# Twelve of a hybrid encoder's input-projection blocks by fifteen products, six more in front, all kept in DRAM until used

## The chip, the cores and the metric

The kernel runs on one core of a Trainium2 chip. Its engines are TensorE (PE, with its weight loads shown as PEld), VectorE (DVE), ScalarE (ACT), GpSimd (POOL) and SyncE (SP), which issues most of the DMA transfers. The metric is the device time of one execution in microseconds (us), the median of several runs. Before the change it is 1644.96 us, of three runs at 1642.6, 1644.96 and 1649.06.

## The reference

One layer of a streaming encoder is computed in float32 for 1024 prompt frames and 32 sample frames, 1056 token columns in all, with a model width of 1024:

```python
h = rmsnorm(x, g_mix) * (1 + sc1) + sh1
u = h @ w_in
qa, ka, va, qm, km, vm, om, ip, fp, ga, gm = split(u)
ya = band_attention(qa, ka, va, rel_bias)      # 8 heads x 64, own chunk and 8 before
conv = silu(causal_conv4(concat(qm, km)))      # width-4 convolution along the tokens
hm = mlstm_chunkwise(conv_q, conv_k, vm, ip, fp, C0, n0, m0)   # 4 heads x 128, a recurrence
ym = head_rmsnorm(hm, mh_gain) * sigmoid(om)
merged = sigmoid(ga) * (ya @ w_br_att) + sigmoid(gm) * (ym @ w_br_mlstm)
x = x + gt1 * (merged @ w_out)
h2 = rmsnorm(x, g_ffn) * (1 + sc2) + sh2
x = x + gt2 * ((silu(g) * up) @ w_down)        # g, up = split(h2 @ w_gate_up)
y = rmsnorm(x, g_final)
```

sh1, sc1, gt1, sh2, sc2, gt2 come from `silu(c) @ w_ada + b_ada`, one row for the prompt and one for the sample. Besides y, the new keys and values, the last rows ahead of the convolution, and the mLSTM state are outputs.

## The kernel before, in words

**Tiling.** All activations lie transposed: model width on the partitions, tokens along the free axis. The 1056 tokens are cut into three thirds of 352 columns (`TILES`, line 24). A block is 128 columns of a weight; its result is one 128 x 1056 row. A matmul multiplies 128 x 128 of the weight with 128 x 352 tokens. Float32 accuracy comes from three passes (`PASSES`, line 41) over high and low halves: weights are split by `split_to` (389 to 395: a copy on ACT gives the high half, a subtraction on DVE or POOL the low one), tokens h too. So a `unit` (421), one block times one third, is 8 x 3 = 24 matmuls, and a block 72.

**Order.** PE, ACT, DVE and POOL run in the order in which the program is written. `Weights` (55) loads raw blocks ahead on SP's queue and splits up to `ahead` blocks before use. `Side` (102) is the pacing: `unit` calls `side.tick()` after every six matmuls, and a job started with so many steps over so many ticks advances by its share. In this way a generator such as `attention(hp)` (638, 22 steps) or `mlstm(pr)` (992, 26 steps, two for each 128 tokens) is laced between the matmuls of plain blocks. The list `segs` gives each segment its plain blocks and its generator:

- k0, v0, q0 alone (k0 and v0 by `first_units`, line 440, which runs two blocks at once while h is made slice by slice)
- attention(0) beside k, v, q of the next pair of heads and 2 gates; attention(1) likewise; attention(2) beside k, v, q and 4 gates
- attention(3) beside vm0 and the convolution blocks 0, 4, 1, 5
- mlstm(0) beside vm1 and the convolution blocks 2, 6, 3, 7
- mlstm(1), then `branch_operands`, beside four output-gate blocks (`om_block`, 1168) and 8 gates

`ada_rest` (1129), the rest of the modulation, is a side job of 160 steps spread over 495 ticks from the second segment on. Gate rows are stored to DRAM by SP (`gate_block`, 590) and loaded in the merge.

**An mLSTM pass.** `first` (1017) makes scores, mask and weighted keys of the next 128 tokens, `scaled` (1088) scales the numerator of the pass before, `weigh` (1042) weighs scores, `second` (1046) computes numerator and new state C and then the scale: reciprocal on DVE (1079), squares on ACT (1082), mean and power on POOL (1084, 1085). `third` (1093) transposes the result.

**Fifteen products.** The FFN's up projection already has a cheaper form. Instead of 3 x 2 x 3 block products (three weight rows, two halves of the model width, three thirds of tokens), fifteen products of sums of weights with sums of tokens are made, each of 4 x 3 = 12 matmuls; `fifteen_products` adds them into three rows. The token sums, called forms, are made first: `early_forms` (48 sums shared by DVE and POOL at line 1563, 24 low halves at 1576) beside a few plain blocks, then `late_forms` (20 low halves) in the first ten products. `times` holds the matmul of line 1726. For these stages the PSUM pools mm and ps (line 428's results, scores) are closed and psb opened, eight banks.

## Time and profile before

| what | value |
|---|---|
| three runs | 1642.6, 1644.96, 1649.06 us |
| profiled execution, its own time | 1642.54 us |
| its span | 1640.6 us |
| granted TensorE clock, mean | 0.995 |
| DMA, mean over the span | 117 GB/s |
| start to the first block's matmuls | 48.4 us |
| k0 and v0 (`first_units`) | 48.4 to 73.6 us |
| q0 | 73.6 to 88 us |
| attention 0, 1, 2, 3 | to 176, 263, 373, 473.6 us |
| mLSTM first and second half, up to the last gates | to 568.5 and 730 us |
| merge, output projection, norm, three plain FFN blocks | to about 1018 us |
| fifteen products of the FFN | 1018 to 1373 us |
| down projection and final norm | to 1640.6 us |

Busy times of an engine are read as shares of a window: an engine with 100% sets its length, one with 60% may still set it by an order of waits. "Idle before" a group of instructions names the instruction that ended the wait. Matmul ends are modelled, so a wait of PE is seen best as a gap between groups.

### The profile page before, as it was taken

What the parts mean: (1) busy time and instruction counts of PE and PEld (TensorE: products, weight loads), DVE (VectorE), ACT (ScalarE), POOL (GpSimd) and SP (SyncE); (2) the same over time, 40 slices, a digit from 0 to 9 for tenths busy, and PEclk for the clock granted to TensorE, in tenths of its full rate; (3) what the DMA queues carried; (4) which work ended last, traced back from release to release, by engine and by line L of the source; (5) the groups of instructions that cost most, each with busy time, mean ns of one, the idle gap of its engine ahead of it and who ended that gap; (6) DMA issues with size and microseconds to landing.
All of it is one profiled execution on the core that took longest, in us unless ns stands there. A gap on an engine that the chain in (4) does not pass through costs nothing.

```text
span 1640.6 us, 27517 instructions
## 1 busy us (share of the span) xinstructions
PE 1589.7 (97%) x10324; PEld 1566.7 (95%) x10324; DVE 1121.0 (68%) x2100; ACT 780.8 (48%) x1732; POOL 535.7 (33%) x540
## 2 busy tenths in 40 slices
PE   7989999999999999999999998999999999999997
PEld 6989999999999999999999988999999999999997
DVE  6756564546776744546655689889888986698754
ACT  3456454543455544444434645454545444444443
POOL 1234333333332311000012155566565742233101
PEclk9999999999999999999999999999999999999999
DMA  9732323232222332584453211313222236427453
GB/s 344 251 98 75 111 75 106 67 126 75 84 83 78 67 94 66 131 273 152 128 151 109 91 53 39 105 53 104 79 82 88 78 102 216 141 65 238 134 157 123
DMA packets 210326, 192.45 MB, mean 117 GB/s; under 512 B 10570, under 2 KB 180530, under 8 KB 209170
## 3 DMA queue, kind: packets, MB, share of 16 engines
q1 hardware_dynamic: 205970, 188.60, 36.8%
q10 hardware_dynamic: 4224, 2.10, 0.4%
q8 instruction: 81, 1.33, 0.4%
q14 instruction: 51, 0.42, 0.1%
HBM read 152.19 MB, written 41.63 MB: 118 GB/s over the span
## 4 chain that ended last, share of the span: by engine, by line
PE 79%; DVE 8%; ACT 3%; issue 2%; DMA 1%; POOL 1%; DVEq 0%; POOLq 0%; ACTq 0%
PE mm L428 35%; PE psb L1726 24%; PE psb L2082 5%; PE mm L825 3%; PE psb L1967 3%; PE psV L725 2%; PE psS L667 1%; DVE wsp L395 1%; PE psT L694 1%; DVE s L395 1%; DVE s L1576 1%; DVE s L1989 1%; DVE sl L1563 1%; DVE st L681 1%; PE psV L1059 1%
## 5 line engine op out<-in xcount | busy, mean ns | idle before, releaser
L428 PE MATMUL mm<-s,wsp 128*128 128x352 f32 x4104 | 690.4, 324 | 5.8 <-DVE t L1657 1.9
L428 PEld LDWEIGHTS mm<-s,wsp 128*128 128x128 f32 x4104 | 656.8, 188 | 9.0 <-DVE stg L518 2.3
L1726 PE MATMUL psb<-s,wsp 128*128 128x352 f32 x2544 | 422.0, 323 | 11.4 <-DVE s L1989 5.5
L1726 PEld LDWEIGHTS psb<-s,wsp 128*128 128x128 f32 x2544 | 410.9, 189 | 14.4 <-issue 6.1
L395 DVE TENSOR_TENSOR wsp<-wraw,wsp 128x512 fp32r<-128x512 f32 (+1 forms) x284 | 246.0, 884 | 136.0 <-ACT wsp L394 134.2
L394 ACT ACTIVATE wsp<-wraw 128x512 fp32r<-128x512 f32 x340 | 201.5, 617 | 147.6 <-PE psb L1726 84.5
L687 POOL TENSOR_SCALAR st<-st,mx 128x640 f32<-128x640 f32 (+5 forms) x72 | 57.0, 791 | 193.7 <-DVE mx L686 179.5
L1141 DVE SCALAR_TENSOR_TENSOR t<-wa,cmix,t 128x512 f32<-128x512 f32 x112 | 88.8, 797 | 8.9 <-DMA wa<-in_w_ada_dram 8.5
L395 POOL TENSOR_TENSOR wsp<-wraw,wsp 128x512 fp32r<-128x512 f32 x56 | 73.8, 1339 | 52.4 <-ACT wsp L394 52.0
L2082 PE MATMUL psb<-s,wsp 128*128 128x352 f32 x528 | 86.7, 324 | 0.0
L2082 PEld LDWEIGHTS psb<-s,wsp 128*128 128x128 f32 x528 | 84.7, 188 | 0.0
L681 DVE CUSTOM_DVE_ANT_0 st<-psS,bias 128x640 f32<-128x640 f32 (+5 forms) x72 | 44.5, 618 | 57.8 <-PE psS L667 44.9
L1726 PE MATMUL psb<-x,wsp 128*128 128x352 f32 x432 | 80.2, 325 | 2.3 <-DVE x L1576 2.3
L682 ACT ACTIVATE st<-st,mx 128x640 f32<-128x640 f32 (+5 forms) x72 | 47.9, 666 | 67.5 <-DVE mx L681 67.5
L1676 POOL TENSOR_TENSOR t<-t,sl 128x352 f32<-128x352 f32 x18 | 17.4, 969 | 185.3 <-ACT sl L1674 185.3
L1726 PEld LDWEIGHTS psb<-x,wsp 128*128 128x128 f32 x432 | 71.5, 189 | 2.8 <-DVE x L1576 2.8
L701 ACT ACTIVATE pT<-psT 128x640 fp32r<-128x640 f32 (+3 forms) x80 | 38.7, 494 | 72.1 <-PE psT L694 55.1
L1764 DVE TENSOR_TENSOR t<-t,psb 128x352 f32<-128x352 f32 x120 | 60.4, 512 | 5.2 <-PE psb L1726 4.8
L1361 POOL TENSOR_TENSOR wraw<-wraw 128x512 f32<-128x512 f32 x25 | 37.1, 1482 | 76.8 <-DVE wsp L395 75.8
L706 DVE TENSOR_TENSOR pT<-psT,pT 128x640 fp32r<-128x640 f32 (+3 forms) x80 | 44.0, 559 | 20.5 <-ACT pT L701 20.4
L1361 POOL TENSOR_TENSOR wraw<-wraw,raw 128x512 f32<-128x512 f32 x33 | 55.8, 1704 | 0.9
L825 PE MATMUL mm<-s,s 128*128 128x264 f32 (+3 forms) x432 | 54.9, 283 | 0.0
(340 smaller groups left out, 2334.2 us busy)
## 6 DMA issues: line engine op xcount, KB each, us to landing
wraw<-in_w_in_dram SPq DMA_DIRECT2D x40, 512.0 KB
wraw<-in_w_gate_up_dram SPq DMA_DIRECT2D x33, 512.0 KB
wa<-in_w_ada_dram SPq DMA_DIRECT2D x64, 256.0 KB
wraw<-in_w_down_dram SPq DMA_DIRECT2D x32, 512.0 KB
a_d<-t SPq DMA_DIRECT2D x22, 528.0 KB
g_d<-t SPq DMA_DIRECT2D x16, 528.0 KB
x<-xres SPq DMA_DIRECT2D x16, 528.0 KB
t<-g_d SPq DMA_DIRECT2D x16, 528.0 KB
```

The lines of the kernel that those rows point to most:

```text
L394: act.activation(dst[:, 0], src, AF.Copy)
L395: eng.tensor_tensor(dst[:, 1], src, f(dst[:, 0]), op=ALU.subtract)
L428: pe.matmul(pt[:, :hi - lo], wt[(w0 + k) // 4][:, a, (w0 + k) % 4], xt[k][:, b, lo:hi], start=(k == 0 and q == 0), stop=(k == n - 1 and q ...
L681: dve.tensor_tensor_reduce(so, sv, bi, -1.0, 3.0e38, ALU.add, ALU.min, mx[:n, 1:2])
L687: pool.tensor_scalar(st[:n, :w], st[:n, :w], mx[:n, 3:4], 1.0, op0=ALU.mult, op1=ALU.mult)
L825: pe.matmul(pt[:n, :wd], hs[k][:, a, i * P:i * P + n], whl[b][:, k, :wd], start=(k == 0 and q == 0), stop=(k == KD - 1 and q == 2))
L1141: dve.scalar_tensor_tensor(ac[:, c], wa, cmix[:, c, k:k + 1], ac[:, c], op0=ALU.mult, op1=ALU.add)
L1361: pool.tensor_tensor(a(dst), a(x), a(y), op=op)
L1726: pe.matmul(acc, wt[:, a, k], x[k][:, b], start=(start and not onto and k == 0 and q == 0), stop=(stop and k == 3 and q == 2), skip_group_ ...
L1764: dve.tensor_tensor(c, c, y, op=ALU.add if sign > 0 else ALU.subtract)
L1967: pe.matmul(acc, wt[k // 4][:, u, k % 4], piece_of[k, i][:, v], start=(k == 0 and q == 0), stop=(k == KP - 1 and q == 2))
L2082: pe.matmul(acc, wt[(k - k0) // 4][:, u, (k - k0) % 4], piece_of[k, 2][:, v], start=(k == 0 and q == 0), stop=(k == NF - 1 and q == 2))
```

## The change

24 blocks of w_in get a new place and a new way: convolution 2, 6, 3, 7, the four output-gate blocks and the 16 merge gates. Their rows go to DRAM (`u_d`, `o_d`, `g_d`), now stored by ACT's queue.

- Six of them come first as plain blocks, two in `first_units` and four beside the forms of h (`Tokens`, the FFN's helper made a class). For these, each normalised x gets its shift added in place (`whole_x`), and one third of it is stored to DRAM (`h_d`), since the forms will overwrite that third of the split h.
- Twelve follow as four times fifteen products (720 matmuls for 864).
- Then the PSUM pools are changed back, the thirds of h are loaded and split again, and k0, v0, q0 begin.
- The six gates that are left stand in the two mLSTM segments: two behind vm1, four beside mlstm(1).
- The segments of attention 0 to 2 hold k, v, q alone. Convolution rows 2, 6, 3, 7 and the output gate are loaded from DRAM. `ada_rest` has a number of steps for each segment, from the first on.
- `on_pool` says where weights' low halves are made: on DVE in the front and in the last segment, on POOL between.

```diff
+    def whole_x(j):
+        x = xns[j]
+        for c, a, b in col_segments(0, T):
+            act.activation(x[:, a:b], x[:, a:b], AF.Identity, bias=sh1[:, c, j:j + 1])
+        act.dma_start(h_d[j], x[:, thirds[1 + j // 4]])
...
-                split_to(t[:, :, :n], raw[:, 4 * i:4 * i + n], pool if (W.done or home is slots) and not hm_n[1] else dve)
+                split_to(t[:, :, :n], raw[:, 4 * i:4 * i + n], pool if on_pool[0] else dve)
...
+    def raw_block(c0, dst, home=None, order=(0, 1, 2), last=lambda: None):
+        w = w_cols(c0, home)
+        def run():
+            raw = tmpt()
+            for lo, hi, pt in units(w, order, last):
+                act.activation(raw[:, lo:hi], pt, AF.Copy)
+            W.advance()
+            act.dma_start(dst, raw)
...
+    def conv_loaded(b):
+        xin, dst = conv_in(b)
+        for c, x, y in col_segments(0, T):
+            sp.dma_start(xin[:, x + 3 + 3 * c:y + 3 + 3 * c], u_d[b][:, x:y])
+        for _ in range(3):
+            yield
+        yield from conv_tail(b, xin, dst)
...
+    def load_convs(bs, ticks, delay):
+        late_conv.append(side.start(chain(*map(conv_loaded, bs)), len(bs) * CONV_STEPS, ticks, delay))
...
+    kept = [(QM + b * P, u_d[b]) for b in (2, 6, 3, 7)] + [(OM + b * P, o_d[b]) for b in range(4)] + gates
+    NFRONT, NROWS = 6, 12
...
-        (nothing, b_qkv(0), None, 0),
-        (nothing, mix(b_qkv(1), b_gates(0, 2)), lambda: attention(0), ATT_STEPS),
-        (nothing, mix(b_qkv(2), b_gates(2, 4)), lambda: attention(1), ATT_STEPS),
-        (nothing, b_qkv(3) + b_gates(4, 8), lambda: attention(2), ATT_STEPS),
+        (nothing, b_qkv(0), None, 0, 36),
+        (nothing, b_qkv(1), lambda: attention(0), ATT_STEPS, 20),
+        (nothing, b_qkv(2), lambda: attention(1), ATT_STEPS, 20),
+        (nothing, b_qkv(3), lambda: attention(2), ATT_STEPS, 20),
         (mlstm_setup, [vm_block(0), conv_block(0), conv_block(4), conv_block(1), conv_block(5)],
-         lambda: attention(3), ATT_STEPS),
-        (open_mls, [vm_block(1), conv_block(2), conv_block(6), conv_block(3), conv_block(7)],
-         lambda: mlstm(0), ML_STEPS),
-        (nothing, [om_block(b) for b in range(4)] + b_gates(8, 16),
-         lambda: chain(mlstm(1), conv_rows(), branch_operands()), ML_STEPS + BR_STEPS + 3),
+         lambda: attention(3), ATT_STEPS, 56),
+        (open_mls, [vm_block(1)] + rest[:2], lambda: mlstm(0), ML_STEPS, 14),
+        (om_loads, rest[2:],
+         lambda: chain(mlstm(1), conv_rows(), branch_operands()), ML_STEPS + BR_STEPS + 3, 0),
...
+    tk = Tokens(hs, xq)
+    first_units([run.w for run in front[:2]])
+    on_pool[0] = False
+    W.ahead = 4
+    tk.job = side.start(tk.early(), 9, 10)
+    def start_late():
+        side.drain(tk.job)
+        tk.job = side.start(tk.late_forms(), 24, 24)
+    for run in front:
+        run()
...
+        fifteen_products(tk, x, rows, third_done)
...
+    for j in range(KD):
+        sp.dma_start(back[j], h_d[j])
+    W.ahead = 2
+    on_pool[0] = True
+    for run in segs[0][1][:2]:
+        first[id(run.w), 0] = unit(run.w, 0, hs, *TILES[0])
+    for j in range(KD):
+        split_to(hs[j][:, :, thirds[1 + j // 4]], back[j])
...
-            ada = side.start(ada_rest(), ADA_STEPS, 495)
+        ada[1] = ada_steps / ticks
...
-            delay = 13 if i >= 5 else 0
+            delay = 13 if i == 5 else 4 if i == 6 else 0
             job = side.start(gen(), steps, ticks - delay - 4, delay)
+        if i == 6:
+            on_pool[0] = False
```

The changed kernel's instructions stand in a new order. Line numbers of the changed kernel differ: its plain matmul is line 448 (428 before), transposes of attention 720 (694), scores 693 (667), mLSTM 1057, 1059, 1087 to 1092 (1026, 1028, 1056 to 1061).

PE, in an attention of wide steps, before: one step of attention (transposes psT, scores psS, values psV) and the plain matmuls mm of a block, three to a row, that follow. `s` are tiles of split activations, `wsp` split weights.

```order
L694 MATMUL psT_3227<-ident,st_3091 128x128 x5
L667 MATMUL psS_3235<-s_1842,s_2458 128x320
L667 MATMUL psS_3235<-s_1842,s_722 128x320
L667 MATMUL psS_3235<-s_1842,s_2458 128x320
L667 MATMUL psS_3235<-s_1842,s_722 128x320
L725 MATMUL psV_3174<-pT_3156,s_2237 128x256 x4
L428 MATMUL mm_3213<-s_582,wsp_2960 128x352 x3
L428 MATMUL mm_3213<-s_607,wsp_2960 128x352 x3
L428 MATMUL mm_3213<-s_633,wsp_2960 128x352 x3
L428 MATMUL mm_3213<-s_665,wsp_2960 128x352 x3
L428 MATMUL mm_3274<-s_479,wsp_2959 128x352 x3
L428 MATMUL mm_3274<-s_505,wsp_2959 128x352 x3
```

The same place of the changed kernel, one step to the next:

```order
L720 MATMUL psT_4674<-ident,st_4616 128x128 x5
L693 MATMUL psS_4682<-s_3656,s_4213 128x320
L693 MATMUL psS_4682<-s_3656,s_2686 128x320
L693 MATMUL psS_4682<-s_3656,s_4213 128x320
L693 MATMUL psS_4682<-s_3656,s_2686 128x320
L751 MATMUL psV_4664<-pT_4646,s_4252 128x256 x4
L448 MATMUL mm_4715<-s_473,wsp_4465 128x352 x3
L448 MATMUL mm_4715<-s_499,wsp_4465 128x352 x3
L448 MATMUL mm_4715<-s_527,wsp_4465 128x352 x3
L448 MATMUL mm_4715<-s_555,wsp_4465 128x352 x3
L720 MATMUL psT_4731<-ident,st_4653 128x128 x5
```

After the step, six rows of plain matmuls (18) or more stood before; now four rows (12) stand between one step and the next.

PE, in the second half of mLSTM, before: the second part of a pass (C, kw and W are state, weighted keys and weights), plain matmuls, and the scores of the next.

```order
L1056 MATMUL psT_6965<-C_6871,s_5630 128x129
L1056 MATMUL psT_6965<-C_6871,s_6067 128x129
L1059 MATMUL psV_6966<-s_5248,kw_6830 128x129 x2
L1061 MATMUL psT_6965<-s_5248,W_6826 128x129 x2
L428 MATMUL mm_6942<-s_633,wsp_6748 128x352 x3
L428 MATMUL mm_6942<-s_665,wsp_6748 128x352 x3
L428 MATMUL mm_6999<-s_479,wsp_6747 128x352 x3
L428 MATMUL mm_6999<-s_505,wsp_6747 128x352 x3
L428 MATMUL mm_6999<-s_531,wsp_6747 128x352 x3
L428 MATMUL mm_6999<-s_556,wsp_6747 128x352 x3
L1026 MATMUL psS_7014<-s_5630 128x128
L1028 MATMUL psS_7014<-ident,s_5630 128x128
```

The same place after, from the scores to the second part:

```order
L448 MATMUL mm_7841<-s_473,wsp_7514 128x352 x3
L448 MATMUL mm_7841<-s_499,wsp_7514 128x352 x3
L1057 MATMUL psS_7850<-s_6671 128x128
L1059 MATMUL psS_7850<-ident,s_6671 128x128
L1057 MATMUL psS_7850<-s_7157 128x128
L1059 MATMUL psS_7850<-ident,s_7157 128x128
L1127 MATMUL mm_7862<-ident,num_7766 128x128 x2
L448 MATMUL mm_7841<-s_527,wsp_7514 128x352 x3
L448 MATMUL mm_7841<-s_555,wsp_7514 128x352 x3
L1087 MATMUL psT_7876<-C_7827,s_6671 128x129
L1087 MATMUL psT_7876<-C_7827,s_7157 128x129
L1090 MATMUL psV_7877<-s_6578,kw_7799 128x129 x2
```

Six rows of plain matmuls (18) stood between second part and scores; now two rows (6) stand ahead of the scores and two behind.

DVE, behind `first_units`, before: the low parts of k0 (line 502), the tails of v0 (518, 546).

```order
L502 TENSOR_TENSOR s_688<-mm_476,s_688 64x352 x2
L502 TENSOR_TENSOR s_688<-mm_477,s_688 64x352 x2
L502 TENSOR_TENSOR s_688<-mm_478,s_688 64x352 x2
L518 COPY stg_757<-mm_755 32x128
L546 TENSOR_TENSOR s_778<-mm_779,s_778 128x8x64
L546 TENSOR_TENSOR s_778<-mm_792,s_778 128x8x64
L518 COPY stg_811<-mm_809 32x128
```

After, at the end of the front stage: line 1486 is a sum of the forms, 1499 a low half of a form, 411 the low half of a weight, and `psb` in the COPY a finished product.

```order
L1486 TENSOR_TENSOR x_51_291<-x_51_291 128x352
L1499 TENSOR_TENSOR s_1021<-sl_1080,s_1021 128x352
L411 TENSOR_TENSOR wsp_1105<-wraw_719,wsp_1105 128x512
L411 TENSOR_TENSOR wsp_1108<-wraw_719,wsp_1108 128x512
L1499 TENSOR_TENSOR s_473<-x_49_289,s_473 128x352
L1499 TENSOR_TENSOR s_499<-x_49_289,s_499 128x352
L411 TENSOR_TENSOR wsp_1196<-wraw_721,wsp_1196 128x512
L411 TENSOR_TENSOR wsp_1199<-wraw_979,wsp_1199 128x512
L1499 TENSOR_TENSOR s_527<-x_49_289,s_527 128x352
L1499 TENSOR_TENSOR s_555<-x_49_289,s_555 128x352
L1639 COPY row_1213<-psb_1219 128x352
```

Low halves of the first products' weights stand between low halves of the late forms, in one queue, ahead of the first product's copy.

More of the change, by code (lines that the diff above doesn't have):

```diff
@@ L1437, in hybrid_stream_step @@
         sp.dma_start(xres[j], xTs[j])
[L1438 to L1440 removed]
+    open_sl()
+    tk = Tokens(hs, xq)
[6 more added lines that the diff above has]
+        tk.job = side.start(tk.late_forms(), 24, 24)
+    for run in front:
+        run()
+    ps_cm.__exit__(None, None, None)
```

497 lines of the change are left out of this document (271 added, 226 removed), and 8 rows, old and new, of the table PARTS.

## The prediction

> **What bounds the kernel now.** I read the page first, then the chain that ended last, then a table of windows by stage, and only then the waits of single stages.
>
> ```profile
> PE 1589.7 (97%) x10324; PEld 1566.7 (95%) x10324; DVE 1121.0 (68%) x2100; ACT 780.8 (48%) x1732; POOL 535.7 (33%) x540
> ```
>
> TensorE (PE) is busy for 1589.7 of 1640.6 us, so at most 51 us of waits are left in the whole span. The chain says what one plain matmul is worth where nothing holds it: the two longest links are runs of products alone.
>
> ```profile
> 709.78 147.50 PE mm L428 x918
> ...
> 1018.85 354.32 PE psb L1726 x2197
> ```
>
> 147.50 / 918 = 0.161 us and 354.32 / 2197 = 0.161 us. That is the unit of the sum: a block of 128 columns is 72 matmuls, 11.6 us. Next the stages (columns: window, length, busy time with instruction count of PE, PEld, DVE, ACT, POOL, then clock, DMA share, GB/s). The windows are q0, the four attentions, and the two mLSTM halves.
>
> ```profile
> 73.60:88.00 14.40, 13.91 (x91) 13.41 (x90) 4.85 (x10) 8.52 (x20) 6.42 (x8) 1.00 0.63 196
> 88.00:176.00 88.00, 83.81 (x556) 79.94 (x555) 53.01 (x129) 48.22 (x111) 33.40 (x42) 1.00 0.26 77
> 176.00:263.00 87.00, 85.91 (x575) 83.08 (x574) 50.98 (x126) 45.04 (x107) 32.12 (x40) 1.00 0.29 89
> 263.00:373.00 110.00, 107.48 (x718) 105.34 (x716) 55.20 (x132) 51.75 (x120) 43.47 (x53) 1.00 0.33 101
> 373.00:473.60 100.60, 98.34 (x707) 95.86 (x708) 71.37 (x192) 48.61 (x113) 33.89 (x50) 1.00 0.23 68
> 473.60:568.50 94.90, 94.90 (x706) 93.25 (x704) 67.95 (x151) 52.85 (x149) 31.08 (x50) 1.00 0.34 85
> 568.50:722.00 153.50, 153.50 (x1013) 151.98 (x1013) 79.47 (x176) 70.69 (x173) 18.29 (x29) 1.00 0.42 118
> ```
>
> PE fills nearly every window. But it fills them with plain blocks that stand beside attention and mLSTM as cover. The change takes 24 of these blocks away to the front. So the question of this case is not only what 144 matmuls save, but where a stage without its cover shows the chain that lay under it.
>
> **The change part by part.** The sum is made on the profiled execution, 1642.54 us, with 1640.6 in the span. Of the three runs shown (1642.6, 1644.96, 1649.06) it stands at the fast end, 2.4 us under the median.
>
> *The gain.* 12 blocks by fifteen products are 4 x 15 x 12 = 720 matmuls in place of 864: 144 x 0.161 = 23.2 us. All other blocks keep their matmuls.
>
> *First units.* In each of eight steps ScalarE now also adds the shift to x and issues a store:
>
> ```profile
> 59.42 1.36 ACT L380 ACTIVATE s<-s,sh 128x1024 fp32r<-128x1024 f32 x2 [1.35 <-issue]
> ...
> 77.62 0.43 ACTq L525 DMA_DIRECT2D out_dram<-stg  x1
> ```
>
> Two passes of at most 1.36 and an issue of 0.43 make 3.15 us a step, against 25.2 / 8 = 3.15 us that a step lasts now (48.4 to 73.6). I take 0.5 us, between 0 and 1.6. The 24 other stores moved to ScalarE's queue cost 24 x 0.43 = 10 us of an engine that is 48% busy, spread over 250 us: nothing.
>
> *The four other plain blocks with the forms beside them.* The same stage exists before the FFN (960 to 1018). Its rows, and those of its operations:
>
> ```profile
> 960.00:1000.00 40.00, 34.36 (x212) 33.44 (x210) 35.14 (x57) 17.97 (x42) 21.96 (x19) 1.00 0.23 75
> 1000.00:1040.00 40.00, 35.87 (x210) 35.12 (x210) 33.62 (x52) 21.77 (x48) 20.80 (x14) 0.91 0.19 59
> 1040.00:1100.00 60.00, 60.00 (x376) 60.00 (x376) 52.85 (x73) 29.85 (x58) 36.42 (x24) 1.00 0.25 81
> ```
>
> ```profile
> L395 DVE TENSOR_TENSOR wsp<-wraw,wsp 128x512 fp32r<-128x512 f32 x268 | 238.1, 905 | 128.4 <-ACT wsp L394 126.5
> L1141 DVE SCALAR_TENSOR_TENSOR t<-wa,cmix,t 128x512 f32<-128x512 f32 x112 | 88.8, 797 | 8.9 <-DMA wa<-in_w_ada_dram 8.5
> L1576 DVE TENSOR_TENSOR s<-sl,s 128x352 fp32r<-128x352 f32 x24 | 14.3, 606 | 0.0
> L1563 POOL TENSOR_TENSOR x<-x 128x352 f32<-128x352 f32 x11 | 12.1, 1109 | 3.5 <-issue 1.7 <-DVE x L1563 1.0 <-DVE t L1563 0.5
> L1563 DVE TENSOR_TENSOR sl<-sl,x 128x352 f32<-128x352 f32 x8 | 7.1, 882 | 4.5 <-POOL sl L1563 4.5
> ```
>
> In the new stage VectorE (DVE) has 24 sums x 0.882 + 24 low parts x 0.606 + 8 weight splits x 0.905 = 43 us, PE 288 x 0.161 = 46.4. Right behind, the first ten products bring 10 x 0.905 + 20 x 0.606 = 21.2 us to DVE against 120 x 0.161 = 19.3 on PE. Both nearly tie, so waits must show; in the two windows before the FFN, PE lost 5.6 + 4.1 = 9.8 us, with a norm beside it that the new stage lacks. I take 7 (bounds: 4.1, the second window's loss, and 13.5, if each of 24 sums waited for the other engine as eight of them did for 4.5 us).
>
> At the end of that stage the PSUM pools change, and there the trace shows a second loss, in the clock:
>
> ```profile
> 1014.14 1.07 PE L1726 MATMUL psb<-s,wsp 128*128 128x352 f32 x5 [1.80 <-DVE wsp L395]
> ...
> 1018.85 0.66 PE L1726 MATMUL psb<-x,wsp 128*128 128x352 f32 x1 [2.33 <-DVE x L1576]
> ```
>
> ```profile
> 1016.00:1020.00 4.00, 1.67 (x6) 1.22 (x6) 4.00 (x6) 0.00 (x0) 2.34 (x2) 0.50 0.00 0
> 1020.00:1024.00 4.00, 4.00 (x21) 4.00 (x20) 3.38 (x8) 2.96 (x7) 0.00 (x0) 0.74 0.44 131
> ```
>
> Granted 0.50 and 0.74, PE loses 0.50 x 1.67 + 0.26 x 4 = 1.9 us of work on top of its gaps. I take 1.9 for the new seam as well, since DVE stands in front of PE there in the same way. [...]
>
> *The second seam*, behind the last product: PSUM goes back to the old pools, and the first unit of k0 needs a bank that ScalarE or DVE has just read. No such change of pools stands behind products in the trace of before. I take 1 us, between 0 and the 2.33 of the gap above.
>
> *Putting h back.* Eight loads stand on SP's queue ahead of the weights of the third block and of w_ada, which wait behind them; eight pairs of copy and subtraction follow. The nearest store and load of the trace:
>
> ```profile
> 368.75 3.85 DMA ya_d<-t
> 372.62 1.61 DMA t<-in_state_conv_dram
> ```
>
> The stores are long done; a load and a split fit under the 48 matmuls (7.7 us) of the two units that need only h's first third. I take 0; without that cover 4. The eight loads of kept convolution rows and the four of the output gate, later on SP's queue, have three free steps or a whole segment before they are used: 0.
>
> *Segment of k0, v0, q0.* Some 28 steps of ada now lie beside 27 us of products, 112 x 0.797 / 160 = 0.56 us of DVE each, 16 us, with the eight splits. I take 1, up to 3 if wa comes late.
>
> *Attention 0 to 2.* The blocks beside them go from 5, 5, 7 to 3. DVE's order contains waits on ScalarE inside one step (exp, then the reciprocal), which do not shrink with the cover. In 88 to 176 these were:
>
> ```profile
> DVE mx L686 <- ACT st L682: 6.9, 15, 0.7
> ...
> DVE t L732 <- ACT t L731: 3.2, 7, 1.4
> ```
>
> So DVE needs 53.0 + 10.1 = 63.1 us for attention 0, PE 83.8 - 23.2 = 60.6: 2.5 us. For attention 1 it is 61.1 against 62.7: 0. For attention 2, 55.2 + 10.1 less the 7 ada steps that leave (84 ticks x 160 / 495 = 27 become 20; 3.9 us) is 61.4 against 107.5 - 46.4 = 61.1: 0.3. I take 3 in all, from 0 to 21.
>
> *Attention 3.* Its blocks stay, but 56 ada steps lie there in place of 19: 37 x 0.56 = 20.7 us more of DVE, 71.4 + 20.7 + 10.1 = 102 against 98.3 on PE. I take 3 (0 to 6).
>
> *mLSTM halves.* Here the trace shows the chain that the blocks covered, two steps of the second half:
>
> ```profile
> 608.40 0.61 PE L1056 MATMUL psT<-C,s 128*128 128x129 f32 x4
> ...
> 609.57 0.60 DVE L1090 TENSOR_SCALAR num<-num,dn 128x128 f32<-128x128 f32 x2
> ...
> 609.65 3.14 PE L428 MATMUL mm<-s,wsp 128*128 128x352 f32 x18
> ...
> 611.77 0.17 DVE L1079 RECIPROCAL dn<-dn 128x2 f32<-128x2 f32 x1
> ...
> 612.03 0.40 ACT L1082 ACTIVATE sq<-num,dn 128x128 f32<-128x128 f32 x1 [1.47 <-DVE dn L1079]
> ...
> 612.63 0.38 PE L1026 MATMUL psS<-s 128*128 128x128 f32 x2
> ...
> 613.14 0.69 POOL L1084 TENSOR_SCALAR dn<-dn 128x2 f32<-128x2 f32 x1 [7.11 <-ACT sq L1082]
> ...
> 613.43 2.81 PE L428 MATMUL mm<-s,wsp 128*128 128x352 f32 x16
> ...
> 614.64 0.60 DVE L1090 TENSOR_SCALAR num<-num,dn 128x128 f32<-128x128 f32 x2 [0.87 <-POOL dn L1085]
> ```
>
> ```profile
> 620.81 0.19 POOL L1084 TENSOR_SCALAR dn<-dn 128x2 f32<-128x2 f32 x1 [6.20 <-ACT sq L1082]
> ```
>
> Scale, new C, numerator, reciprocal, square on ScalarE, power on POOL, scale again: 614.64 - 609.57 = 5.07 us, or 4.57 where the POOL step takes 0.19 for 0.69. PE's own share of a pass is 1.25 (608.40 to 609.65) + 0.80 (612.63 to 613.43) = 2.05 us. Now 36 matmuls and more fill a pass of 8 us, so nothing shows. In the changed second half, 41 steps go over 40 ticks of six matmuls: a pass has 12 x 0.161 + 2.05 = 3.98 us of PE. With a loop of 4.95, PE waits 1 us in each of 8 passes: 8 us (0 to 13). In the first half the ticks beside vm1 last 0.75 us:
>
> ```profile
> 473.60:568.50 94.90, 26.99 (x216) 25.53 (x216) 1.00 0.34 85
> ```
>
> (the vm1 matmuls alone: 27 us for 36 ticks). 26 steps over 43 ticks give a pass 3.3 x 0.75 + 2.05 = 4.5 us; (4.95 - 4.5) x 7 passes = 3 us (0 to 7).
>
> *Sum.* 0.5 + 7 + 1.9 + 1 + 0 + 1 + 3 + 3 + 8 + 3 = 28.4 against 23.2: 1642.54 + 5.2 = 1647.7. The median of before lies 2.4 above its profile; I add half, **1649 us**. A measurement of this kernel can tell about 0.5% from no change, 8.2 us: faster is below 1636.7, slower above 1653.2. The forecast is no change, a little on the slow side. Its own range, from the costs' nearer bounds, is 1638 to 1659.
>
> **The rivals.** *R1, the cover was not needed.* The stages before had DVE idle by 30% and more, steps of attention run three deep, and the products of 1040 to 1100 keep PE at 60 of 60 with DVE at 52.85. Then the loop in mLSTM closes in under 4 us because ScalarE and POOL have less beside it, attention packs into the shorter segments, and only the front (8.9), first units (0.5), second seam (1) and some 2 us are paid: 1642.5 - 23.2 + 12.4 = 1631.7, 1632 us (1626 to 1637). Against it stands the measured loop.
>
> *R2, VectorE holds attention* (this ends slower). The wide steps already show it:
>
> ```profile
> 290.00:310.00 20.00, 18.38 (x126) 17.92 (x125) 12.95 (x27) 11.86 (x26) 8.69 (x10) 1.00 0.25 70
> ```
>
> 1.62 us lost in four steps (22 steps in 110 us), 0.4 a step, with all the cover there. It decides once a step's order on DVE takes longer than PE's 60.6 / 22 = 2.75 us. At 0.4 in each of 66 steps, 26.4 less the 4.2 + 1.1 + 2.5 lost already, it is 18.6 in place of 3, and 6 in place of 3 in attention 3: 1649 + 18.6 = 1668 us. Against it: DVE's mean need, 63.1 / 22 = 2.87, is hardly above the line.
>
> *R3, VectorE and GpSimd shut each other out in the forms.* If their times add up, the front has 43 + 24 x 1.109 = 69.6 us against PE's 46.4, 23.2 in place of 7: 1665 us. Against it the rows: 52.85 + 36.42 = 89.3 us busy within 60, and 35.14 + 21.96 = 57.1 within 40. [...]
>
> **How the numbers follow.** Forecast 0.42 (faster 0.02, same 0.28, slower 0.12), R1 0.38 (faster 0.34, same 0.04), R2 0.15 and R3 0.05 (slower). Faster 0.36, same 0.32, slower 0.32. Range: from R1's low end, 1626, to R2's middle, 1668; about 0.07 lies below and 0.1 above.
>
> **What would show it.** Right: about 10,180 PE instructions; waits of PE in the second mLSTM half for the state's scale or its numerator, about 1 us a pass; 7 us of waits and a clock below 1 around the seam of the front; nothing at the reload of h. Wrong: PE full in both mLSTM halves (R1), PE waiting for DVE in the scores and transposes of attention by over 5 us a segment (R2), DVE instructions of the front longer than in the rows above (R3). A long wait for a load from DRAM in any segment would be a case that I have not priced.

## The result, and the profile after

The changed kernel takes 1757.71 us (median of four runs, 1754.77 to 1759.23), the kernel before 1643.78 (median of four runs, 1641.88 to 1649.06). The ratio of the means is 1.0685, 95% interval 1.0655 to 1.0716. It is 114 us slower; the forecast was 1649, with a range up to 1668.

The page's first line for the changed kernel:

```profile
PE 1614.3 (92%) x10180; PEld 1576.5 (90%) x10180; DVE 1252.9 (71%) x2290; ACT 832.0 (47%) x1830; POOL 611.6 (35%) x594
```

The 144 matmuls are gone, yet PE is busy 24.6 us longer, and idle for 140 us of 1754.5 in place of 51. At 0.161 us a matmul the remaining work is 1589.7 - 23.2 = 1566.5 us, so 48 us of "busy" are put down to matmuls at a lower clock (the mean granted clock is 0.966, 0.995 before), and 89 us are new waits. The stages of the changed kernel, from the front blocks to the stretch behind the last gate (columns as before: window, length, busy time of PE, PEld, DVE, ACT, POOL, then clock, DMA share, GB/s). They are the front, the fifteens, k0-v0-q0, attention 0 to 3, the two mLSTM halves, and that stretch:

```profile
74.70:129.00 54.30, 49.08 (x290) 48.52 (x288) 43.62 (x58) 23.43 (x54) 29.47 (x27) 0.94 0.31 105
129.00:254.40 125.40, 118.39 (x721) 116.82 (x721) 96.36 (x144) 55.27 (x109) 65.53 (x42) 0.97 0.30 96
254.40:306.60 52.20, 42.03 (x238) 40.18 (x239) 29.20 (x49) 16.47 (x35) 15.21 (x14) 0.90 0.60 189
306.60:391.80 85.20, 69.36 (x428) 64.81 (x427) 59.74 (x136) 42.41 (x99) 27.90 (x36) 0.90 0.23 71
391.80:473.70 81.90, 68.81 (x425) 63.92 (x424) 52.10 (x126) 39.96 (x96) 28.16 (x36) 0.92 0.27 80
473.70:558.10 84.40, 69.29 (x424) 63.90 (x423) 50.56 (x126) 41.42 (x99) 31.08 (x38) 0.92 0.19 59
558.10:671.30 113.20, 105.25 (x726) 100.90 (x726) 85.13 (x217) 49.82 (x116) 41.87 (x63) 0.97 0.26 80
671.30:752.90 81.60, 73.60 (x551) 70.23 (x550) 59.17 (x146) 51.42 (x137) 22.85 (x46) 0.98 0.43 117
752.90:830.20 77.30, 71.81 (x470) 68.72 (x470) 39.04 (x113) 47.45 (x131) 10.77 (x21) 0.96 0.46 95
830.20:843.40 13.20, 2.12 (x15) 1.83 (x13) 3.33 (x4) 3.66 (x5) 0.00 (x0) 0.71 1.00 370
```

To compare, the windows of before were cut again at the first matmul of each segment; the three attentions, which the comparison needs most:

```profile
87.60:176.90 89.30, 85.11 (x564) 81.24 (x564) 53.01 (x129) 48.44 (x111) 33.40 (x42) 1.00 0.27 80
176.90:262.70 85.80, 84.71 (x567) 81.88 (x567) 50.98 (x126) 44.95 (x106) 32.12 (x40) 1.00 0.28 86
262.70:374.40 111.70, 107.90 (x721) 105.77 (x719) 55.20 (x132) 52.48 (x121) 44.67 (x54) 1.00 0.33 102
```

Less the work that left them (144, 144 and 288 matmuls), they should have lasted 66.1, 62.6 and 65.3 us. They last 85.2, 81.9 and 84.4. In the same way, window less moved work against window after:

| stretch | should last | lasts | lost |
|---|---|---|---|
| front, four blocks (288 x 0.161) | 46.4 | 54.3 | 7.9 |
| fifteens (720 x 0.161) | 115.9 | 125.4 | 9.5 |
| k0, v0, q0 (14.0 for q0, two blocks more) | 37.2 | 52.2 | 15.0 |
| attention 0, 1, 2 | 194.0 | 251.5 | 57.5 |
| attention 3 | 99.8 | 113.2 | 13.4 |
| mLSTM, first half | 71.0 | 81.6 | 10.6 |
| mLSTM, second half | 68.8 | 77.3 | 8.5 |
| behind the last gate | 0 | 13.2 | 13.2 |

With 1 us at the start these are 136.7 us, less the gain of 23.2: 113.5, where the two spans differ by 113.9. Before and behind these stretches the two kernels run alike.

What PE waits for in attention 0 to 2 of the changed kernel (engine and line, released by; total us, times, longest):

```profile
PE psT L720 <- DVE pT L732: 14.7, 16, 2.3
PE psS L693 <- DVE mx L707: 9.1, 4, 3.4
PE psS L693 <- DVE s L671: 7.0, 1, 7.0
PE psV L751 <- DVE t L759: 6.7, 9, 2.2
```

In the kernel before, no line of that list is over 1.6 us. Its longest, and the one that answers to the first line above:

```profile
PE mm L428 <- DVE stg L518: 1.6, 1, 1.6
...
PE psT L694 <- DVE pT L706: 0.4, 1, 0.4
```

And one such wait from the timeline of attention 1 (start, length, engine, line; at the end the wait before it and its releaser):

```profile
426.57 1.31 DVE L1172 SCALAR_TENSOR_TENSOR t<-wa,cmix,t 128x512 f32<-128x512 f32 x1
...
427.92 0.82 DVE L707 CUSTOM_DVE_ANT_0 st<-psS,bias 128x640 f32<-128x640 f32 x1
...
428.67 0.82 DVE L732 TENSOR_TENSOR pT<-psT,pT 128x640 fp32r<-128x640 f32 x1
...
429.63 1.30 PE L720 MATMUL psT<-ident,st 128*128 128x128 f32 x5 [2.34 <-DVE pT L732]
```

PE's next transposes wait until VectorE has taken the low part of the last ones. VectorE is not short of time, it is in the middle of its queue: a step of the modulation (L1172), then the scores, then the low part. Before, 18 plain matmuls or more (2.9 us) stood between two steps; now there are 12 (1.9 us). The clock falls in the same place:

```profile
429.00:430.00 1.00, 0.37 (x2) 0.40 (x3) 0.75 (x3) 1.00 (x3) 0.01 (x1) 0.72 0.00 0
430.00:431.00 1.00, 1.00 (x8) 0.96 (x7) 0.55 (x1) 0.22 (x2) 0.93 (x1) 0.50 0.81 202
431.00:432.00 1.00, 1.00 (x8) 1.00 (x7) 0.62 (x3) 0.94 (x2) 0.21 (x1) 0.50 1.20 337
432.00:433.00 1.00, 1.00 (x6) 0.96 (x5) 0.66 (x3) 0.62 (x3) 0.25 (x1) 0.57 1.07 309
```

A wait of 2.34 us is followed by some 3 us at half the clock: the five transposes behind it take 1.30 us. By these rows PE loses 1.5 us of work to the clock on top of the wait. It is not so behind every wait: of the nine waits of over 1.5 us in these three segments, seven were followed by such a stretch, among them all three of 2.34 us, and two were not (1.92 us ahead of 460.92, 2.19 us ahead of 553.39). Over the three segments PE is idle 35 us longer than before and its own work takes 22 us longer; over the whole kernel it is 89 and 48.

### The profile page after: what moved, and what is told of

It reads as the page before. It is cut to its first block, busy times and chain, and to the rows that moved or that the text cites. A ratio compares the mean times of both kernels' runs of the same rounds, so it can differ in the third digit from the quotient of the medians.

```text
span 1754.5 us, 27752 instructions
## 1 busy us (share of the span) xinstructions
PE 1614.3 (92%) x10180; PEld 1576.5 (90%) x10180; DVE 1252.9 (71%) x2290; ACT 832.0 (47%) x1830; POOL 611.6 (35%) x594
## 4 chain that ended last, share of the span: by engine, by line
PE 59%; DVE 18%; ACT 7%; DMA 7%; issue 4%; POOL 3%; SPq 1%; ACTq 0%; DVEq 0%; POOLq 0%
PE psb L1605 28%; PE mm L448 16%; PE psb L2197 5%; PE psb L2082 3%; DVE t L1172 2%; DVE wsp L411 2%; DVE s L1499 2%; DVE st L707 2%; DMA rb_d<-in_rel_bias_dram 1%; PE mm L839 1%; DVE sl L1486 1%; ACT st L708 1%; DMA wa<-in_w_ada_dram 1%; PE psT L720 1%; DVE s L1012 1%
## 5 line engine op out<-in xcount | busy, mean ns | idle before, releaser
L448 PE MATMUL mm<-s,wsp 128*128 128x352 f32 x3240 | 568.2, 331 | 20.0 <-ACT t L620 11.1
L448 PEld LDWEIGHTS mm<-s,wsp 128*128 128x128 f32 x3240 | 534.6, 194 | 24.7 <-ACT t L620 11.4
L1605 PE MATMUL psb<-s,wsp 128*128 128x352 f32 x3120 | 519.0, 324 | 13.9 <-DVE s L2104 5.4
L1605 PEld LDWEIGHTS psb<-s,wsp 128*128 128x128 f32 x3120 | 504.9, 189 | 17.6 <-DVE wsp L411 6.9
L411 DVE TENSOR_TENSOR wsp<-wraw,wsp 128x512 fp32r<-128x512 f32 (+1 forms) x314 | 278.8, 903 | 117.3 <-ACT wsp L410 114.9
L1605 PE MATMUL psb<-x,wsp 128*128 128x352 f32 x576 | 107.6, 325 | 7.3 <-ACT x L1496 4.8
L1605 PEld LDWEIGHTS psb<-x,wsp 128*128 128x128 f32 x576 | 95.4, 189 | 8.5 <-ACT x L1496 5.1
L1172 DVE SCALAR_TENSOR_TENSOR t<-wa,cmix,t 128x512 f32<-128x512 f32 x112 | 91.6, 842 | 8.9 <-DMA wa<-in_w_ada_dram 8.3
L1643 DVE TENSOR_TENSOR t<-t,psb 128x352 f32<-128x352 f32 x160 | 80.7, 513 | 14.4 <-PE psb L1605 14.3
L2197 PE MATMUL psb<-s,wsp 128*128 128x352 f32 x528 | 86.7, 324 | 0.0
L2197 PEld LDWEIGHTS psb<-s,wsp 128*128 128x128 f32 x528 | 84.7, 188 | 0.0
L411 POOL TENSOR_TENSOR wsp<-wraw,wsp 128x512 fp32r<-128x512 f32 x42 | 59.2, 1433 | 56.4 <-ACT wsp L410 56.0
L720 PE MATMUL psT<-ident,st 128*128 128x128 f32 x240 | 40.1, 290 | 23.7 <-DVE pT L732 18.3
L411 DVE TENSOR_TENSOR wsp<-raw,wsp 128x512 fp32r<-128x512 f32 x56 | 56.4, 1006 | 7.7 <-ACT wsp L410 7.1
## 6 DMA issues: line engine op xcount, KB each, us to landing
s<-in_w_ada_dram SPq DMA_DIRECT2D x8, 1024.0 KB, 11.5
```

The source lines that it names most:

```text
L411: eng.tensor_tensor(dst[:, 1], src, f(dst[:, 0]), op=ALU.subtract)
L448: pe.matmul(pt[:, :hi - lo], wt[(w0 + k) // 4][:, a, (w0 + k) % 4], xt[k][:, b, lo:hi], start=(i == 0 and q == 0), stop=(i == n - 1 and q ...
L720: pe.transpose(pT[:, b * P:(b + 1) * P], st[:, b * P:(b + 1) * P], ident)
L1172: dve.scalar_tensor_tensor(ac[:, c], wa, cmix[:, c, k:k + 1], ac[:, c], op0=ALU.mult, op1=ALU.add)
L1605: pe.matmul(acc, wt[:, a, k], x[k][:, b], start=(start and not onto and k == 0 and q == 0), stop=(stop and k == 3 and q == 2), skip_group_ ...
L1643: dve.tensor_tensor(c, c, y, op=ALU.add if sign > 0 else ALU.subtract)
```

## The experiments

Two theories were at hand. Theory 1: the plain blocks were cover, and without them the chain PE, ScalarE, VectorE, PE of each step shows, together with the clock. The rival: other parts of the change cost the time (the modulation's steps, which it crowds into fewer ticks; transfers; stores). Each kernel below was run once with a profile; the kernel before took 1642.16 us beside the first three (the gates moved, useless cover, the modulation out of attention 0 to 2) and 1651.69 us beside the others. A total of one run is therefore uncertain by some 10 us, and the readings go by windows. A kernel with the 22 steps of attention alone, which would have measured the chain by itself, gave no time: in that order its instructions wait for each other without end. So the length of the chain alone was not measured.

**Cover taken away alone, in the kernel before.**

```diff
-        (nothing, b_qkv(0), None, 0),
-        (nothing, mix(b_qkv(1), b_gates(0, 2)), lambda: attention(0), ATT_STEPS),
-        (nothing, mix(b_qkv(2), b_gates(2, 4)), lambda: attention(1), ATT_STEPS),
-        (nothing, b_qkv(3) + b_gates(4, 8), lambda: attention(2), ATT_STEPS),
+        (nothing, b_qkv(0) + b_gates(0, 8), None, 0),
+        (nothing, b_qkv(1), lambda: attention(0), ATT_STEPS),
+        (nothing, b_qkv(2), lambda: attention(1), ATT_STEPS),
+        (nothing, b_qkv(3), lambda: attention(2), ATT_STEPS),
...
-        if i == 1:
+        if i == 0:
             ada = side.start(ada_rest(), ADA_STEPS, 495)
```

> The kernel before, with one thing changed: the eight gate blocks that stood beside attention 0 to 2 run alone, straight behind q0. Nothing by fifteen products, no forms, no reload, the modulation's steps at the same rate. Theory 1 (missing cover): attention 0 to 2 with k, v, q alone take 82 to 86 us each as in the changed kernel (85.2, 81.9, 84.4) with a granted clock of 0.90 to 0.92; with 8 x 11.6 = 93 us for the gates the kernel is about 1643 + 93 + 251 - 285 = 1702 us. Rival (the waits in attention come from what else the change brought: stores on ScalarE's queue, the earlier steps of the modulation, DRAM traffic): each takes 63 to 67 us at a full clock, and the kernel stays at 1640 to 1652 us.

It took 1686.46 us. Its attention 0 to 2:

```profile
187.40:259.30 71.90, 64.43 (x425) 59.98 (x424) 42.46 (x116) 40.16 (x95) 24.21 (x34) 0.98 0.23 73
259.30:336.80 77.50, 65.20 (x416) 60.30 (x416) 47.24 (x118) 39.99 (x96) 27.12 (x36) 0.96 0.24 71
336.80:414.60 77.80, 68.19 (x424) 62.98 (x424) 45.12 (x120) 41.59 (x99) 28.44 (x36) 0.93 0.18 54
```

Neither forecast was met: 227.2 us where 194.0 are work, 33 lost, between the 57.5 of theory 1 and the rival's nothing. With no fifteens, reload or moved store in the kernel, missing cover alone costs 33 us there, at a rate of 12 steps of the modulation a segment; the changed kernel has 20. (The modulation starts one segment earlier here, to keep its rate; q0, with its first steps beside it, lasts 20.5 us for 14.0.)

**Useless cover put back into the changed kernel.**

```diff
     def units(w, order=(0, 1, 2), last=lambda: None):
...
+            if id(w) in dummy:
+                unit(w, 0, hs, lo, hi, False)
             yield lo, hi, unit(w, 0, hs, lo, hi) if done is None else done
...
-        ticks = sum(4 * run.w[2] for run in blocks)
+        ticks = sum(4 * run.w[2] for run in blocks) + (24 if 1 <= i <= 3 else 0)
```

(`dummy` holds k and v of the pairs 1 to 3.)

> The changed kernel, with the six units of k and v in attention 0 to 2 made twice, the first time into PSUM that nobody reads: 144 useless matmuls (23.2 us) a segment, and the pacing told of the 24 extra ticks. Theory 1 (a chain through ScalarE and VectorE sets these segments, and the clock falls in the waits): a segment goes from 82 to 85 us to at most 89, the clock back to 0.98 or more, the kernel to 1757 to 1772 us. Rival (PE's own work plus fixed stalls at the head of a segment): each segment grows by 15 to 23 us, the kernel to 1803 to 1827 us.

It took 1773.56 us, 1.6 over the upper end for theory 1 and 29 below the rival's range.

```profile
307.20:399.30 92.10, 87.55 (x571) 84.94 (x570) 59.10 (x136) 42.70 (x99) 27.46 (x36) 0.96 0.21 66
399.30:485.20 85.90, 84.48 (x568) 81.83 (x567) 50.76 (x126) 40.32 (x96) 28.55 (x36) 1.00 0.25 77
485.20:572.10 86.90, 85.02 (x569) 81.80 (x567) 51.12 (x126) 41.54 (x99) 32.16 (x38) 1.00 0.17 54
```

69.6 us of work were added, and the three windows grew by 13.4. They last 264.9 us for 194.0 + 69.6 = 263.6 of work: the loss of 57.5 is down to 1.3, with the same 20 steps of the modulation, now spread over more matmuls, and the same queues and transfers. Attention 0 alone missed its forecast: 92.1 us at a clock of 0.96, where at most 89 at 0.98 were expected. In attention 1, PE's own work is 84.48 - 23.2 = 61.3 us here and 68.81 without the cover: so some 7.5 us of that window were clock.

**The modulation's steps out of attention 0 to 2**, and then **VectorE's share of them alone**.

```diff
-        (nothing, b_qkv(1), lambda: attention(0), ATT_STEPS, 20),
+        (nothing, b_qkv(1), lambda: attention(0), ATT_STEPS, 0),
...
+    def dve_only():
+        t = ada_tile()
+        dve.memset(t, 1.0)
+        for _ in range(14):
+            dve.scalar_tensor_tensor(t, t, gt1[:, 0, 0:1], t, op0=ALU.mult, op1=ALU.max)
+            yield
...
+        if 1 <= i <= 3:
+            side.start(dve_only(), 14, ticks)
```

(The first edit, made in all three segments, is in both kernels; the rest only in the second.)

> The changed kernel without the 20 steps of the modulation in each of attention 0 to 2; the 54 that are then left run uncovered behind the last segment, so only the three windows count, not the total. Theory 1 (latency of the chain): each window shortens by 0 to 4 us, as the steps lie mostly where VectorE waits. Rival 2 of the prediction as it was worded (VectorE's own load of 63 us holds attention): each shortens by about 20 x 0.56 = 11 us.

> The changed kernel with the modulation's steps out of attention 0 to 2, and in their place 14 useless VectorE instructions of the same size (128 x 512, about 0.8 us, 11 us a segment) paced over the segment: no transfers, no GpSimd, no matmul with them. The steps' removal took the three windows from 85.2, 81.9, 84.4 to 78.0, 74.1, 72.9. If VectorE's time is what they cost, the windows come back to 82 to 86. Rival (the transfers of w_ada, GpSimd's part and the small matmuls behind them cost it): they stay within 2 us of 78, 74 and 73.

The windows without the steps, and with VectorE's instructions in their place:

```profile
304.70:382.70 78.00, 64.99 (x420) 60.52 (x420) 47.40 (x118) 42.36 (x99) 23.15 (x34) 0.93 0.17 50
382.70:456.80 74.10, 65.14 (x415) 60.17 (x415) 39.40 (x108) 39.90 (x96) 24.41 (x34) 0.95 0.20 61
456.80:529.70 72.90, 63.02 (x417) 57.62 (x415) 39.30 (x108) 41.38 (x99) 27.04 (x36) 1.00 0.13 39
```

```profile
305.30:387.40 82.10, 66.96 (x419) 62.35 (x419) 58.34 (x133) 42.41 (x99) 26.70 (x34) 0.92 0.16 48
387.40:465.70 78.30, 66.66 (x416) 61.73 (x415) 50.77 (x123) 39.91 (x96) 27.70 (x34) 0.93 0.19 57
465.70:545.20 79.50, 67.08 (x418) 61.83 (x416) 49.44 (x122) 41.41 (x99) 30.54 (x36) 0.94 0.12 36
```

The steps' removal gave back 7.2, 7.8 and 11.5 us: the first two lie between the forecasts, the third meets the 11 us of rival 2. 31 of the 57.5 us stayed. VectorE's time alone took 4.1, 4.2 and 6.6 of it again, 14.9 of 26.5. Only attention 0, at 82.1, came back to what VectorE's time alone would give; the other two lie between the forecasts. The useless instructions make 32.4 of the 36.3 us of VectorE's busy time that the steps had made. So a little over half of the cost is VectorE's time; the rest is in the steps' other parts, which were not told apart.

**The modulation's steps at the two ends.** In the changed kernel, k0-v0-q0 was given none (36 before) and attention 3 was given 20 (56 before).

```diff
-        (nothing, b_qkv(0), None, 0, 36),
+        (nothing, b_qkv(0), None, 0, 0),
...
-         lambda: attention(3), ATT_STEPS, 56),
+         lambda: attention(3), ATT_STEPS, 20),
```

> The changed kernel with no steps of the modulation beside k0, v0, q0 (36 before) and 20 in place of 56 beside attention 3; the rest runs uncovered at the end of the segments, so only the two windows count. If these steps' loads and VectorE time cause the extra time there, k0-v0-q0 goes from 52.2 to 40 to 44 us and attention 3 from 113.2 to 101 to 105. Rival (the reload of h and the missing order around it hold the first; attention's chain the second): 49 to 53 and 109 to 113 us.

The two windows:

```profile
252.70:293.90 41.20, 38.55 (x231) 37.55 (x232) 10.01 (x20) 16.63 (x35) 11.47 (x12) 0.96 0.50 162
...
536.20:635.40 99.20, 98.79 (x710) 96.10 (x710) 69.56 (x187) 50.02 (x117) 36.59 (x59) 1.00 0.21 62
```

11.0 and 14.0 us less: all of attention 3's loss, and most of the first segment's. The first is within its forecast, the second 1.8 us below it (20 steps are also fewer than the 27 of the kernel before). Attention 0 to 2, which the edit left at 20 steps each, lasted 83.6, 78.3 and 80.4 us here, 9.2 us less in all than in the changed kernel. So where in a segment the parts of these steps fall seems to matter too; no run tested that.

**The same crowding in the kernel before.**

```diff
+        if i == 4:
+            ada[1] = 56 / 60
+        if i == 5:
+            ada[1] = 38 / 204
```

> The kernel before with the modulation's steps paced as the change has them in one place: 56 in attention 3 in place of 19 (and fewer later). Cover, blocks and everything else stay. If crowding these steps is the cause there, attention 3 goes from 99.8 to 107 to 114 us and the kernel to 1650 to 1658 us. Rival (in the changed kernel something else of that segment costs it): at most 102 us, and 1640 to 1648.

It took 1678.10 us, and attention 3:

```profile
376.00:509.90 133.90, 113.50 (x735) 107.89 (x735) 102.69 (x242) 47.70 (x111) 40.22 (x55) 0.91 0.30 93
```

34 us more, far over the forecast of 7 to 14. Part of that is my count: the segment has 84 ticks, not 60 (vm0 makes 36 of them), so 78 steps ran there, and 27, not 19, in the kernel before. 51 more steps cost 34 us, 0.67 each. VectorE's load, 102.69 us, is now above the 98.8 us of PE work, and yet it fills only 77% of the window: here too the total does not set the time. PE is idle for 20.4 us, and its longest waits are the modulation's own. Every twenty steps end in eight small matmuls that stand in PE's queue and wait for VectorE (`PE mm L1153 <- DVE t L1148: 7.3, 2, 4.1`). The changed kernel has the same wait: `PE mm L1184 <- DVE t L1179`, 5.0 us beside k0-v0-q0 and 3.6 in attention 3.

**Three transfers moved.** The bias (`rb_d`, 3 MB) goes out from ScalarE's queue behind the first fifteen; six of the eight thirds come back into tiles of the pool tmp; x is loaded in the merge by ScalarE's queue.

```diff
-        sp.dma_start(rb_d, bass.AP(rel_row.tensor, rel_row.offset, [[FLEN, H], [0, P], [1, FLEN]]))
...
+        if i == 0:
+            act.dma_start(rb_d, bass.AP(rel_row.tensor, rel_row.offset, [[FLEN, H], [0, P], [1, FLEN]]))
...
-        t = f(ap_.tile([P, 2, WIN], F32R, tag="pT", name=nm("back")).rearrange("p s c -> p (s c)"))
+        t = tmpt()
...
-        sp.dma_start(x2[j], xres[j])
+        act.dma_start(x2[j], xres[j])
```

> The changed kernel with three transfers taken out of the way: the relative bias goes to DRAM from ScalarE's queue behind the first fifteen products, not from SP's beside first_units; six of eight thirds of h come back into tiles of another pool, which are free before the last products end; and the residual x is loaded from ScalarE's queue in the merge, not ahead of attention's rows on SP's. If the traced waits are the cause, PE starts the third front block at once (5 us less between 74.7 and 79.7), k0-v0-q0 shortens by 4 to 10 us, and the stretch behind the last gate by 9 to 12 us: the kernel at 1731 to 1740 us. Rival (each wait only uncovers the next one: weights, the last row's store): less than 8 us in all, 1750 to 1758.

It took 1740.50 us, half a microsecond over the forecast; by the spans 15.8 less, 1738.7 for 1754.5. What the first one is about, in the changed kernel:

```profile
79.15 1.18 ACT L620 ACTIVATE t<-mm 128x352 f32<-128x352 f32 x3 [6.29 <-DMA rb_d<-in_rel_bias_dram]
...
79.66 14.11 PE L448 MATMUL mm<-s,s 128*128 128x352 f32 x72 [4.69 <-ACT t L620]
```

And with the transfer moved:

```profile
76.14 11.73 PE L448 MATMUL mm<-s,s 128*128 128x352 f32 x72
87.72 34.86 PE L448 MATMUL mm<-s,wsp 128*128 128x352 f32 x216
```

ScalarE's queue stood for a transfer that SyncE had issued (what ties the two is not shown); PE waited 4.69 us for ScalarE to empty a bank, and then ran its next block at a granted clock of 0.82 (79.66 to 93.77: 14.11 us for 72 matmuls, 11.73 without the wait). Without it, the four front blocks take 11.73 + 34.86 = 46.6 us, at a clock of 1.00 (75 to 125 us). k0-v0-q0 goes from 52.2 to 47.7 us, and the wait behind the last gate, in the changed kernel this one,

```profile
839.22 1.08 ACT L410 ACTIVATE s<-t 128x1056 fp32r<-128x1056 f32 x1 [9.53 <-DMA t<-ya_d]
...
843.39 3.01 PE L448 MATMUL mm<-s,wsp 128*128 128x352 f32 x9 [11.08 <-ACT t L620]
```

shortens from 11.08 to 4.58 us, 6.5 us where 9 to 12 were expected: there too ScalarE's queue stood behind a load, with the copies that empty PSUM behind it, as seven loads of x were ahead of attention's rows.

**Six blocks by fifteens**, with the other gates back beside mLSTM, then the same with the other repairs, in two forms.

```diff
-    NFRONT, NROWS = 6, 12
+    NFRONT, NROWS = 6, 6
...
-        (open_mls, [vm_block(1)] + rest[:2], lambda: mlstm(0), ML_STEPS, 14),
-        (om_loads, rest[2:],
+        (open_mls, [vm_block(1)] + rest[:4], lambda: mlstm(0), ML_STEPS, 14),
+        (om_loads, rest[4:],
```

> The changed kernel with six blocks by fifteen products in place of twelve; the other six gates go back beside mLSTM (two more in the first half, four more in the second). The fifteens shorten by 63 us, plain work grows by 70. Theory 1 (the recurrence of 4.6 to 5 us a pass sets the mLSTM halves, and their blocks hide it): the first half goes from 81.6 to 92 to 97 us, the second from 90.5 (with the stretch behind it) to 118 to 128, the kernel to 1733 to 1747 us. Rival (no slack there): 1762 to 1768 us.

The second kernel has, with these and the three transfers moved, the modulation's steps late. The numbers of steps by segment, from the first on, in the changed kernel and in this one:

```diff
-36, 20, 20, 20, 56, 14, 0
+20,  0,  0,  0, 20, 45, 80
```

> All that helped so far in one: six blocks by fifteens, gates back beside mLSTM, the modulation's steps away from attention 0 to 2 and from half of k0-v0-q0 and attention 3 into the mLSTM halves (45 and the rest), and the three transfers moved. By adding the parts up: 1740 - 22 (attention 0 to 2) - 22 (transfers) - 8 (attention 3) = about 1688 us, 1675 to 1705. It stays slower than the kernel before, since attention still lacks its cover: by theory 1 some 10 us in each of three segments, and the front gives back 7. If it came under 1650 us, theory 1 would have the wrong size for what cover is worth.

The third has them thin, again as numbers by segment:

```diff
-36, 20, 20, 20, 56, 14, 0
+12, 10, 12, 12, 28, 36, 60
```

> The six blocks by fifteens once more, with the three transfers moved and the modulation's steps thinned everywhere, none crowded: 12 beside k0-v0-q0, 10 to 12 in attention 0 to 2, 28 in attention 3, 36 and the rest in the mLSTM halves. By the windows: 1742 - 17 (transfers) - 9 (first segment) - 10 (attention 0 to 2) - 9 (attention 3) + 8 + 15 (mLSTM halves) = 1720 us, 1708 to 1732. Under 1650 would speak against the cost of missing cover; over 1736 would say that these steps cost the same wherever they stand.

The first took 1741.89 us, as theory 1 had it, but not by its parts. The two halves:

```profile
608.60:712.50 103.90, 97.17 (x693) 93.51 (x693) 61.73 (x146) 58.82 (x149) 30.14 (x50) 0.98 0.43 116
712.50:826.30 113.80, 113.80 (x760) 112.08 (x759) 49.35 (x124) 58.24 (x152) 10.76 (x21) 1.00 0.51 142
```

The first half was expected at 92 to 97 us; the second, with the stretch behind it, at 118 to 128. In the second half PE is full, its loss of 8.5 us is gone, and so is the long wait behind the last gate. The first half has its four blocks again and still takes 103.9 us for the 94.2 of before: its loss of 10 us is not missing cover. (What it is stays open. PE's longest waits there, 4.7 us in four, are for VectorE's weighted scores, `PE psS L1057 <- DVE W L1075`, and VectorE in turn waits for ScalarE's weighted keys, `DVE W L1075 <- ACT kw L1069: 10.6, 4, 4.8`. The convolution tails now run in other places, which no run took back.) The second took 1735.89 us, 31 over its range: with the modulation's steps put into them, the mLSTM halves lasted 11 and 32 us longer (114.8 and 145.4). The third, with all steps thin, took 1715.59 us as expected, against 1651.69 for the kernel before. It is the fastest version found, and 4% slower than before in one run of each.

## Why the prediction was wrong, point by point

The costs were put at 28.4 us and came to 136.7; 57.5 of these lie in attention 0 to 2.

- **The gain** is as stated: 10324 - 10180 = 144 matmuls.
- **The step that failed** is attention 0 to 2: "DVE needs 53.0 + 10.1 = 63.1 us for attention 0, PE 83.8 - 23.2 = 60.6: 2.5 us", and 3 us in all. It set two totals against each other, as if each engine ran on its own. But a step goes round PE, ScalarE, VectorE and back to PE, in queues that are filled in a fixed order; when the plain matmuls between steps are fewer than that way takes, PE waits, although VectorE is idle for 30 to 40% of these windows. 3 us became 57.5. The runs show it from both sides: 33 us lost with cover taken away alone, 1.3 left with useless cover put back. R2 named the place, the direction and the sign (PE's waits for VectorE in scores and transposes, over 5 us a segment, are 30.8 us in three); its price, 18.6 us, was made from waits of the kernel before, where the cover still stood, and its condition (VectorE's mean need over PE's) was again one of totals.
- **The clock** was counted at one seam, 1.9 us. By the busy times it is 48 us of the loss, since in attention 0 to 2 seven of the nine waits of over 1.5 us were followed by some 3 us at about half of it. What was one term belongs to every term that has waits.
- **The modulation's steps** were put at 1 us in k0-v0-q0 and 3 in attention 3. They cost 11.0 and 14.0 there, and 26.5 of the 57.5 in attention 0 to 2. In attention 3 the sum was even stated (102 us of VectorE against 98.3 of PE) with an upper bound of 6; the step count was wrong (27 before, not 19; with 27 the same sum gives 97.7 us, and no loss at all), but the size was missed because the bound again added totals.
- **Putting h back** at 0 to 4 us: the loads had to wait until the last rows of the fifteens were stored (`SPq L1732 <- DMA g_d<-row: 2.9, 1, 2.9`), whose memory they go to. VectorE stood 7.8 us for them (`DVE s L411 <- DMA back<-h_d: 7.8, 1, 7.8` in the waits of that window), ahead of k0's low parts. Of the segment's 15 us, 4.5 went when the loads were moved (this and the 11.0 of the modulation's steps overlap).
- **The front** was put at 7 us for VectorE and 1.9 for the clock. VectorE kept up: 46.6 us for 46.4 of work once the bias transfer was moved. The 7.9 measured were almost all that transfer (a wait of 4.69 us) and the clock behind it (14.11 - 11.73 = 2.4 us). The products lost more than forecast, 9.5 us from the first to the last. The centre of that is one wait near their start, `PE psb L1605 <- ACT x L1496: 4.8, 1, 4.8`, in the windows of the changed kernel:

```profile
145.00:149.00 4.00, 1.88 (x11) 1.30 (x9) 4.00 (x4) 0.00 (x0) 4.00 (x3) 1.00 0.00 0
149.00:153.00 4.00, 0.12 (x1) 0.12 (x1) 4.00 (x7) 1.06 (x3) 1.40 (x2) 0.57 0.00 0
153.00:157.00 4.00, 3.96 (x14) 3.51 (x15) 3.44 (x8) 2.52 (x6) 0.00 (x0) 0.58 0.48 131
```

  VectorE is full there for 8 us with low halves of forms and weights, as the prediction said ("21.2 us to DVE against 120 x 0.161 = 19.3 on PE"), ScalarE waits for them, and PE all but stops. Part of that time may be GpSimd's doing: the low halves of weights begun at 144.73 and 147.94 us, while GpSimd made sums of weights, took 1.76 and 1.75 us, the one at 151.83, after them, 0.68. With the forms' low halves that is some 3.7 us of the 8, by an estimate from these rows; no run took GpSimd's sums away there.
- **The mLSTM halves** were put at 8 + 3 us and lost 8.5 + 10.6. In the second half the size came out, by luck. The loop is there, and the scales follow each other 4.6 us apart,

```profile
790.56 0.60 DVE L1121 TENSOR_SCALAR num<-num,dn 128x128 f32<-128x128 f32 x2 [1.72 <-POOL dn L1116]
795.17 0.60 DVE L1121 TENSOR_SCALAR num<-num,dn 128x128 f32<-128x128 f32 x2 [1.72 <-POOL dn L1116]
```

  but PE's work of a pass, its 12 plain matmuls included, is 4.4 us (786.99 to 791.38), not 3.98, so a steady pass waits 0.2 us and not 1. The loss is one wait of 2.29 us early on (for VectorE's weighted scores) with a granted clock of 0.70 from 776 to 780 us behind it, and waits of 1.03 and 1.76 us for the scale behind the last passes. That cover hides it was right: with four more gates beside it PE was full again. In the first half neither size nor cause was right.
- **A long wait for a load** behind the last gate (13.2 us) was named as a case not priced; it came, since loads of x went ahead of attention's rows.
- **R1** (the cover was not needed) had the largest chance for a gain and is refuted. **R3** fell on its place, the plain blocks of the front, where PE ran full; but VectorE's instructions did take longer beside GpSimd's, 1.76 and 1.75 us for 0.68 at the seam, and as told below.

## What to carry to other kernels

Work that stands beside a chain of small steps is worth more than its matmuls: before moving it, take the way of one step round all its engines, in the order of their queues, and compare it with the work that is left between two steps, not busy totals. Add to the sum of expected waits about half of it again for the clock (48 us beside 89 here), and look at what else the change paces, since a side job that cost next to nothing under cover cost 26.5 us without it. Ask of every transfer that a reorganised kernel may start early whose queue it holds up.
